# Turning the latents between two layers of a diffusion block: strided engine writes in layer 0, or a trip through DRAM at the layer boundary

## Chip, cores and metric

One core of one Trainium2 chip runs the whole program as one launch. The metric is the device time of an execution in microseconds (us); smaller is better.

## What is computed

Two layers of a hybrid diffusion block run over 512 latent tokens (a grid of 8 rows by 64 columns, read row by row) and 256 context tokens, with 1024 features each. Layer 0 mixes with gated linear attention (GLA) and a gated spatial product (gMLP); layer 1 mixes with a Mamba-2 scan (SSD) that reads the latents column by column. Each layer ends with a SwiGLU feed-forward net (FFN). The reference turns the tokens around layer 1's mixer alone:

```python
def to_col_major(x):
    bsz, t, d = x.shape
    rows = t // GRID_W
    return x.reshape(bsz, rows, GRID_W, d).transpose(0, 2, 1, 3).reshape(bsz, t, d)
...
    for i in range(DEPTH):
        ...
        hx = modulate(rms_norm(x, norm_g[i, 0]), mx[0], mx[1])
        hc = modulate(rms_norm(ctx, norm_g[i, 0]), mc[0], mc[1])
        if i % 2 == 0:
            yx, yc = mixer_gla_gmlp(hx, hc, ...)
        else:
            yx_cm, yc = mixer_ssd(to_col_major(hx), hc, ...)
            yx = to_row_major(yx_cm)
        x = x + mx[2] * yx
        x = x + mx[5] * swiglu(modulate(rms_norm(x, norm_g[i, 1]), mx[3], mx[4]), ffn_w_in[i], ffn_w_out[i])
```

Residual, norms and FFN act on each token alone, so the turn may stand at any place between layer 0's mixer and layer 1's.

## The kernel before, in words

Tokens lie in six tiles of 128: tiles 0 to 3 are latents, tiles 4 and 5 context. All products run in float16 with split operands (high x high, high x low, low x high), so three matmuls of TensorE (PE) stand for one. The program notes its operations in program order and a planner (`Plan`) puts them into an order per engine by a list schedule over its own estimated costs; PE, VectorE (DVE), ScalarE (ACT) and the one DMA queue of SyncE (SP) then run their lists in order. Nearly every instruction carries the line number of the planner's issue loop (562), so the rows below tell them apart by tile names and shapes: `area` is the big on-chip working area, `bank` a PSUM bank, `gran` and `stg` hold weights, `small` a tile's norm sums.

Layer 0 works on row-major tokens up to the ends of its two branches. There the results become the output projection's operand `aT_a` (GLA) and `aT_b` (gMLP), features in partitions and tokens in columns, in two float16 parts: ACT writes the high part, DVE the low part. The kernel before writes the latents' columns in column-major order at that point. For GLA this is one 128x512 write per engine and latent tile (4 tiles); for gMLP one per engine and block of features (4 blocks):

```python
            hi, lo = (t[:, :, XS].rearrange("p h (c r) -> p h r c", r=8)[:, :, 2 * i:2 * i + 2, :] for t in aT_a)
```

Neighbouring elements of such a write lie 8 elements, 16 bytes, apart; the context tiles, and every other write, are contiguous. The residual tiles X[0] to X[3] are loaded in column-major order, and from there on all is column-major.

Layer 0's FFN ends with a product per tile and half, 12 in all, each followed by `resid` (DVE: multiply by the gate, add to X). The tiles come in the order 0 to 5. After each pair, `norm_tiles` makes the pair's operand of layer 1, `hT3`: on ACT the sum of squares and the scaling, on DVE the reciprocal root (`rstd_of`), 16 transposes of 128x128 on PE, then modulation and the split in two parts shared by ACT and DVE. Layer 1 starts with the step sizes (`wd`, 64 wide) and group 0 of four groups: projections with `conv_tile`, whose result goes into one of two padded tiles `pads` and through five taps of a convolution on DVE, context and latents together. `Xd` keeps the residual in DRAM until layer 1's output projection.

Of the kernel before, what the change touches and what calls it, by code (L numbers as in the profile page):

```python
# [19 lines left out]
P = 128  # L20
# [17 lines left out]
class View:  # L38
    """Part of an on-chip tile: partitions p0:p1 and (count, step in bytes) per free dimension from byte off."""
# [57 lines left out]
    def host(self, fn, shape):  # L97
        """The same memory through any view of the tile itself."""
        dims = tuple((n, 0) for n in shape[1:])
        return self._with(("host", fn), p0=0, p1=shape[0], dims=dims)  # L100
# [27 lines left out]
class Base:  # L128
    """An allocated tile; whole: any two uses of it count as overlapping."""
# [24 lines left out]

class Part(Base):
    """A tile of a pool: the scheduler gives it one of the pool's slots, from its first use to its last."""
# [10 lines left out]
class Line:  # L167
    """Tiles in program order: the first one without a slot, and how many before it hold theirs."""
# [13 lines left out]
class Pool:  # L182
    """Equal slots (tile, offset), maybe shared with an earlier pool.

    A pool holds no more than `most` slots. Of these, and of the slots that pools share, so many are kept for the tiles
    that come next in program order that some operation can always go on.
    """
# [39 lines left out]
class Plan:  # L227
    """Instructions are noted in program order, ordered by a list schedule over their estimated times, then issued."""
# [68 lines left out]
    def _note(self, op, hist, box, write, pool, bank=False):  # L297
        """A use of a box depends on the earlier uses that overlap it; uses of one pool do not block each other, and of a
        PSUM bank reads do."""
# [54 lines left out]
    def schedule(self, rounds):  # L354
        """Orders the operations: list schedules by the length of what follows, then by the latest starts that the
        schedule before allows; the shortest is taken."""
# [143 lines left out]
    def _slots(self, op, t):  # L500
        """None when every tile that the operation begins can have a slot at t, else when to look again (-1: unknown)."""
# [19 lines left out]
    def _needs(self):  # L521
        """How many tiles of a pool live at once in program order, when each one begins and soon after."""
# [51 lines left out]
def tile_hybrid_block(ctx: ExitStack, tc: tile.TileContext, t_in: dict, out: bass.AP):  # L574
# [19 lines left out]
    class Ring:  # L594
        """Slots of one size, taken in turn."""
# [115 lines left out]
    def w_rows(w, f0, k0=0, slots=(None,) * 4):  # L711
        """A block of 512 columns for each of 8 slices of the contraction."""
# [4 lines left out]
    def split_pair(w, c0, c1, slots=None):  # L717
        """Two blocks of 128 columns as the rows of A: A11, A12, A22, S1 = A21 + A22, S2 = S1 - A11, S3 = A11 - A21,
        S4 = A12 - S2."""
# [40 lines left out]
    def prod_quarter(o, w, x, sl, more=False):  # L760
        """more: on top of what the bank holds, sums that other engines read or wrote among it."""
# [19 lines left out]
    # ---- 1 / sqrt(ss * scale + eps): a guess from the halved exponent, a cubic and a quadratic step in q = v y y, both  # L781
    # without the factors that the scale of v takes up; y is negative until the last step turns it ----
# [19 lines left out]
    # Rows of 32 partitions go through four column groups of the tensor engine side by side.  # L802
# [22 lines left out]
    def turned(o, n):  # L825
        """The rows of the four groups as columns: (P, group, block of 128, row)."""
# [8 lines left out]
    def mods_cols(layer, chunk, streams):  # L835
        """A chunk of the modulation as columns, the sums over the partitions on the tensor engine."""
# [27 lines left out]
    def mods_row(layer, chunk, streams):  # L864
        """A gate as a row in DRAM per stream, with the scale of the products taken out."""
# [32 lines left out]
    def turn(xs, abv, s, put):  # L898
        """Normalised pairs of tiles as modulated columns, by blocks of 128 features; one engine reads a bank."""
        xn = norm_rows(xs)  # L900
# [19 lines left out]
    def norm_tiles(xs, abv, s, hT, m):  # L920
        ts = [t2[0]((P, 2, 2, P)) for _ in range(4)]
        turn(xs, abv, s, lambda kt: ts[kt // 2][:, kt % 2])
# [3 lines left out]
    class Pairs:  # L926
        """A feature-major operand, the tokens by pairs of tiles."""
# [10 lines left out]
    class Halves:  # L938
        """A feature-major operand in the quarters of Winograd's form of Strassen's product: B11, B21, B22 and the sums
        T1 = B12 - B11, T3 = B22 - B12, T2 = B22 - T1, T4 = B21 - T2; rows halved by feature, columns by tile parity;  # L940
        the tiles by pairs."""
# [10 lines left out]
    def norm_halves(xs, abv, s, hS, m):  # L952
        t = hS.temps((P, 2, 4, 2, P))
        turn(xs, abv, s, lambda kt: t[:, kt // 4, kt % 4])
# [16 lines left out]
    c_rows = t_in["ctx"][0]  # L971

    # =============================== layer 0, mixing ===============================
# [15 lines left out]
    for i in range(NT):  # L989
        sy.dma_start(out=x_in[i], in_=t_in["x"][0][i * P:(i + 1) * P, :] if i < 4 else c_rows[(i - 4) * P:(i - 3) * P, :])  # L990
# [17 lines left out]
    def cols_early(chunk, half):  # L1008
        """Half a shift or scale of both streams: (P, stream, block of 128)."""
# [16 lines left out]
    # The loads in the order of their use: half of shift and scale, the first weights, the other half, the other chunks.  # L1026
# [50 lines left out]
    # Gates: the rows of the low rank side as high, low, high parts and ones, the weights' as high, high, low parts and biases.  # L1077
# [130 lines left out]
    # spatial gating  # L1208
# [27 lines left out]
    for j in range(4):  # L1236
        wu = w_cols(w_in, 1568 + j * P, P)
        for sl in (XS, CS):
# [6 lines left out]
            hi, lo = aT_b[0][:, j, sl], aT_b[1][:, j, sl]  # L1245
            if sl is XS:
                hi, lo = (t.rearrange("p (c r) -> p r c", r=8) for t in (hi, lo))
                u = u.rearrange("p (r c) -> p r c", r=8)
            sc.activation(out=hi, in_=u, func=AF.Copy)
            va.tensor_tensor(out=lo, in0=u, in1=hi, op=ALU.subtract)  # L1250
# [7 lines left out]
    for i in range(NT):  # L1258
# [19 lines left out]
        if i < 4:  # L1278
            src = o.rearrange("p h (a c) -> p h a c", a=2)
            hi, lo = (t[:, :, XS].rearrange("p h (c r) -> p h r c", r=8)[:, :, 2 * i:2 * i + 2, :] for t in aT_a)  # L1280
        else:
            src = o
            hi, lo = (t[:, :, TOK[i]] for t in aT_a)
        sc.activation(out=hi, in_=src, func=AF.Copy)
# [492 lines left out]
```

## Time and profile before

| | |
|---|---|
| median of 3 runs | 1633.5 us (1630.48 to 1634.7) |
| profiled execution, first to last instruction (span) | 1628.5 us |
| median less span (start, end and run-to-run difference) | 5.0 us |
| PE busy | 1576.2 us, 97% of the span |
| DVE busy | 1394.6 us, 86% |
| ACT busy | 955.8 us, 59% |
| granted TensorE clock, mean over the span | 0.991 |

The profiled execution is one execution; its span leaves out what lies ahead of the first and behind the last instruction, so its own time is 1628.5 us plus that rest. Busy time of PE is modelled from pipelined matmuls. Times in rows count from the start of the span.

### The profile page before, as it was taken

How to read it: one execution, taken by the hardware profiler on the slowest of the kernel's cores; microseconds unless marked ns; L12 is line 12 of the kernel's file. 1: busy time of each engine (PE TensorE's matmuls, PEld its weight loads, DVE VectorE, ACT ScalarE, POOL GpSimd, SP SyncE). 2: the span in 40 equal slices, each digit the busy share in tenths (PEclk: the TensorE clock that was granted, in tenths of full speed). 3: DMA queues.
4: the chain of work that ended last, by engine and by line, in shares of the span. 5: the costliest groups of instructions: out<-in, count | busy, mean ns of one | idle time of the engine just before them, and what ended most of it. 6: DMA issues, size and time to landing. Idle time of an engine off the chain costs nothing.

```text
span 1628.5 us, 28131 instructions
## 1 busy us (share of the span) xinstructions
PE 1576.2 (97%) x10893; PEld 953.9 (59%) x10893; DVE 1394.6 (86%) x2661; ACT 955.8 (59%) x1900; POOL 21.4 (1%) x65
## 2 busy tenths in 40 slices
PE   5999989999999999999999999999999999999997
PEld 4555555467545554555569555555544587686774
DVE  3899988689999988966478999999999888898775
ACT  6957437265514622623456899889986576464541
POOL 2000000000000000000000000000000000000000
PEclk8999989999999999999999999999999999999999
DMA  9763335014545566421231455445576324343311
GB/s 329 216 186 113 103 96 156 33 40 126 162 147 162 168 196 192 143 66 59 78 105 47 135 149 148 119 117 153 139 229 186 86 86 128 118 124 113 113 53 52
DMA packets 206121, 210.53 MB, mean 129 GB/s; under 512 B 27199, under 2 KB 154275, under 8 KB 205987
## 3 DMA queue, kind: packets, MB, share of 16 engines
q1 hardware_dynamic: 205987, 208.74, 42.7%
q8 instruction: 85, 1.39, 0.3%
q14 instruction: 49, 0.40, 0.1%
HBM read 197.01 MB, written 7.50 MB: 126 GB/s over the span
## 4 chain that ended last, share of the span: by engine, by line
PE 54%; DVE 23%; ACT 11%; DMA 9%; issue 3%; SPq 0%; DVEq 0%; ACTq 0%
PE bank L562 54%; DVE area L562 15%; ACT area L562 7%; DVE gran L562 5%; DMA stg<-in_ffn_w_in_dram 4%; DMA area<-in_mod_w_dram 2%; DVE stg L562 2%; ACT gran L562 2%; DVE small L562 1%; ACT L562 1%; ACT L560 1%; DMA area<-in_mod_b_dram 1%; SPq L562 0%; DMA area<-rowd 0%; DMA stg<-in_ssd_w_out_dram 0%
## 5 line engine op out<-in xcount | busy, mean ns | idle before, releaser
L562 PE MATMUL bank<-area,gran 128*128 128x256 f16 (+3 forms) x5604 | 789.2, 296 | 3.4 <-DVE area L562 1.8
L562 PEld LDWEIGHTS <-gran 128*128 128x128 f16 x5604 | 519.9, 98 | 252.1 <-issue 19.9
L562 PE MATMUL bank<-area 128*128 128x512 f16 (+9 forms) x3170 | 542.7, 328 | 10.7 <-DVE area L562 5.3
L562 PEld LDWEIGHTS <-area 128*128 128x128 f16 (+1 forms) x3270 | 303.1, 98 | 316.0 <-issue 22.9
L562 ACT ACTIVATE gran<-stg 128x512 f16<-128x512 f32 (+2 forms) x366 | 252.1, 700 | 231.5 <-PE bank L562 96.4
L562 ACT ACTIVATE area<-area 128x128 f32<-128x128 f32 (+8 forms) x557 | 254.1, 502 | 134.6 <-DVE area L562 118.8
L562 DVE TENSOR_TENSOR area<-area 128x512 f32<-128x512 f32 (+8 forms) x489 | 302.1, 641 | 22.8 <-ACT area L562 19.3
L562 ACT ACTIVATE area<-bank 128x384 f32<-128x384 f32 (+7 forms) x460 | 212.2, 482 | 175.7 <-PE bank L562 137.8
L562 DVE SCALAR_TENSOR_TENSOR gran<-stg,gran 128x512 f16<-128x512 f32 (+2 forms) x366 | 278.2, 777 | 32.8 <-ACT gran L562 32.0
L562 PE MATMUL bank<-gran,area 128*128 128x512 f16 (+1 forms) x1308 | 285.7, 361 | 2.0 <-DVE area L562 1.7
L562 DVE TENSOR_TENSOR area<-bank,area 128x512 f32<-128x512 f32 (+5 forms) x237 | 143.2, 612 | 65.1 <-PE bank L562 62.7
L562 DVE SCALAR_TENSOR_TENSOR area<-area,cs 128x512 f32<-128x512 f32 x224 | 159.9, 745 | 10.7 <-DMA area<-in_mod_w_dram 10.0
L562 PEld LDWEIGHTS bank<-area 128*64 128x64 f32 (+4 forms) x1208 | 75.2, 151 | 39.8 <-issue 15.9
L562 DVE SCALAR_TENSOR_TENSOR area<-area,mrow 128x772 f32<-128x772 f32 (+1 forms) x96 | 91.0, 970 | 0.6 <-ACT area L562 0.5
L562 ACT ACTIVATE area<-stg 128x1024 f16<-128x1024 f32 (+1 forms) x56 | 55.0, 998 | 40.1 <-PE bank L562 18.6
L562 DVE SCALAR_TENSOR_TENSOR area<-stg,area 128x1024 f16<-128x1024 f32 (+1 forms) x56 | 64.2, 1153 | 10.0 <-ACT area L562 9.7
L562 ACT ACTIVATE area<-area,small 128x64 f32<-128x64 f32 (+2 forms) x161 | 61.8, 459 | 13.9 <-DVE small L562 13.8
L562 PE MATMUL bank<-ident,area 128*128 128x128 f32 (+1 forms) x351 | 54.0, 294 | 15.3 <-DMA area<-in_ssd_norm_g_dram 5.5
L562 DVE TENSOR_TENSOR stg<-stg,stg 128x512 f32<-128x512 f32 x88 | 60.5, 687 | 1.6 <-DMA stg<-in_ffn_w_in_dram 1.0
L562 PEld LDWEIGHTS bank<-ident,area 128*128 128x128 f32 (+1 forms) x351 | 43.9, 151 | 29.1 <-POOL area L562 5.5
L562 DVE TENSOR_TENSOR stg<-stg 128x512 f32<-128x512 f32 x88 | 60.2, 685 | 0.3
L562 DVE SCALAR_TENSOR_TENSOR area<-area 64x128 f32<-64x128 f32 (+3 forms) x148 | 52.8, 400 | 4.7 <-ACT area L562 4.3
(74 smaller groups left out, 573.2 us busy)
## 6 DMA issues: line engine op xcount, KB each, us to landing
area<-in_mod_w_dram SPq DMA_DIRECT2D x96, 512.0 KB, 3.9
stg<-in_ffn_w_in_dram SPq DMA_DIRECT2D x88, 512.0 KB, 4.4
stg<-in_ffn_w_out_dram SPq DMA_DIRECT2D x44, 512.0 KB, 3.6
stg<-in_ssd_w_in_dram SPq DMA_DIRECT2D x40, 512.0 KB, 3.6
area<-rowd SPq DMA_DIRECT2D x32, 512.0 KB, 5.0
stg<-in_ab_w_in_dram SPq DMA_DIRECT2D x20, 512.0 KB
stg<-in_ssd_w_out_dram SPq DMA_DIRECT2D x32, 256.0 KB, 2.9
area<-in_x_dram SPq DMA_DIRECT2D x8, 512.0 KB, 4.6
```

Of the source, the lines that this page charges most:

```text
L560: eng.preload_act_table_set(TABLE_SETS[table])
L562: getattr(eng, method)(*map(real, a), **{n: real(v) for n, v in k.items()})
```

## The change

Layer 0's two branches write their operands contiguously, all residual tiles are loaded as they lie, and layer 0 stays row-major. The last FFN chunk of layer 0 takes the context tiles first (`last=(4, 5, 0, 1, 2, 3)`). Each finished latent tile is normalised by itself (`norm_rows`), and stored to a DRAM tensor `Xn`, its residual to `Xd`; both stores go to column-major rows (`rows(i)`: 2 grid rows of 64 tokens, 4 KB each). When all four are done, the normalised latents are loaded back as column-major tiles over X (`columns(k)`), and transposed, modulated and split in two pairs. `conv_tile` works on the context ahead of the latents. Layer 1's residual is loaded from `Xd.columns(i)`.

```diff
+class Turned(Base):
+    def _view(self, p0, p1, fn):
+        return View(self, p0, p1, 0, ((D, 4),), F32, (("host", fn),))
+
+    def rows(self, i):
+        return self._view(32 * i, 32 * i + 32, lambda ap: ap.rearrange("(c r) d -> r c d", r=8)[2 * i:2 * i + 2])
+
+    def columns(self, i):
+        return self._view(0, P, lambda ap: ap[P * i:P * i + P])
...
-    def norm_tiles(xs, abv, s, hT, m):
+    def norm_tiles(xn, abv, s, hT, m):
...
-            hi, lo = aT_b[0][:, j, sl], aT_b[1][:, j, sl]
-            if sl is XS:
-                hi, lo = (t.rearrange("p (c r) -> p r c", r=8) for t in (hi, lo))
-                u = u.rearrange("p (r c) -> p r c", r=8)
-            sc.activation(out=hi, in_=u, func=AF.Copy)
-            va.tensor_tensor(out=lo, in0=u, in1=hi, op=ALU.subtract)
+            split(u, [t[:, j, sl] for t in aT_b])
...
-        if i < 4:
-            src = o.rearrange("p h (a c) -> p h a c", a=2)
-            hi, lo = (t[:, :, XS].rearrange("p h (c r) -> p h r c", r=8)[:, :, 2 * i:2 * i + 2, :] for t in aT_a)
-        else:
-            src = o
-            hi, lo = (t[:, :, TOK[i]] for t in aT_a)
-        sc.activation(out=hi, in_=src, func=AF.Copy)
-        va.tensor_tensor(out=lo, in0=src, in1=hi, op=ALU.subtract)
+        split(o, [t[:, :, TOK[i]] for t in aT_a])
...
-        sy.dma_start(out=X[i], in_=x_cm[16 * i:16 * i + 16] if i < 4 else c_rows[(i - 4) * P:(i - 3) * P, :])
+        sy.dma_start(out=X[i], in_=x_rows(i))
...
-    Xd = [scratch((P, D), F32, f"Xd{i}") for i in range(4)]
+    Xd, Xn = (Turned(dram.tile([SEQ, D], F32, name=n)) for n in ("Xd", "Xn"))
...
-                 [k * KB for k in range(96, 120, 4)], gate5):
-        if i % 2:
-            norm_tiles(X[i - 1:i + 1], ab[1, 0], int(i >= 4), hT3, i // 2)
+                 [k * KB for k in range(96, 120, 4)], gate5, last=(4, 5, 0, 1, 2, 3)):
         if i < 4:
-            sy.dma_start(out=Xd[i], in_=X[i])
+            with pl.rushed(20.0):
+                sy.dma_start(out=Xn.rows(i), in_=norm_rows(X[i:i + 1])[0])
+            sy.dma_start(out=Xd.rows(i), in_=X[i])
+        if i == 3:
+            for k in range(4):
+                sy.dma_start(out=X[k], in_=Xn.columns(k))
+            for k in (0, 2):
+                norm_tiles(X[k:k + 2], ab[1, 0], 0, hT3, k // 2)
+        if i == 5:
+            norm_tiles(norm_rows(X[4:6]), ab[1, 0], 1, hT3, 2)
...
-        for sl, o0 in ((XS, 2), (CS, 518)) if with_ctx else ((XS, 2),):
+        for sl, o0 in ((CS, 518), (XS, 2)) if with_ctx else ((XS, 2),):
...
-        sy.dma_start(out=X[i], in_=Xd[i])
+        sy.dma_start(out=X[i], in_=Xd.columns(i))
```

What the planner makes of it stands in the order per engine. On SP's queue, at the end of layer 0's FFN, the kernel before has the four stores of the residual among weight loads:

```order
L562 DMA stg3_75<-in_ssd_w_in_dram 128x2x512
L562 DMA Xd1_124<-area_71 128x1024
L562 DMA stg1_73<-in_ssd_w_in_dram 128x8x128
L562 DMA Xd0_123<-area_71 128x1024
L562 DMA Xd2_125<-area_71 128x1024
L562 DMA area_71<-in_ssd_a_log_dram 128x64
L562 DMA Xd3_126<-area_71 128x1024
L562 DMA area_71<-in_ssd_conv_w_dram 120x128
```

At the same place the changed kernel has:

```order
L576 DMA stg1_73<-in_ssd_w_in_dram 128x8x128
L576 DMA Xd_123<-area_71 2x64x1024 x2
L576 DMA Xn_124<-area_71 2x64x1024 x2
L576 DMA Xd_123<-area_71 2x64x1024 x2
L576 DMA area_71<-in_ssd_a_log_dram 128x64
L576 DMA Xn_124<-area_71 2x64x1024 x2
L576 DMA area_71<-Xn_124 128x1024 x4
L576 DMA area_71<-in_ssd_conv_w_dram 120x128
L576 DMA stg2_74<-in_ssd_w_in_dram 128x8x128
```

The four stores and four loads of `Xn` are new, and the loads stand ahead of the next weight loads of layer 1. On PE, behind the last product of layer 0's FFN, the kernel before goes straight on to the latents of group 0's first projection (weights `gran1`):

```order
L562 LDWEIGHTS area_71
L562 MATMUL bank4_67<-area_71 128x512
L562 LDWEIGHTS gran1_77
L562 MATMUL bank7_70<-area_71,gran1_77 128x256
```

In the changed kernel the context columns of four projections (96 matmuls 256 wide) and of the step sizes (48 matmuls 64 wide) stand there, with the last transposes of the context pair ahead of them; their end, and the latents' transposes behind it, read:

```order
L576 LDWEIGHTS gran5_81
L576 MATMUL bank5_68<-area_71,gran5_81 128x256
L576 MATMUL bank4_67<-ident_94,area_71 128x128 x4
L576 MATMUL bank6_69<-ident_94,area_71 128x128 x4
L576 MATMUL bank0_63<-ident_94,area_71 128x128 x4
L576 LDWEIGHTS gran1_77
L576 MATMUL bank4_67<-area_71,gran1_77 128x256
```

All latent work of layer 1 has moved behind the transposes of the reloaded tiles, and PE has nothing else in its list between the last `gran5` matmul and those transposes.

## Rows read from the trace of the kernel before

**Rows 1.** The page: busy time of each engine.
```profile
PE 1576.2 (97%) x10893; PEld 953.9 (59%) x10893; DVE 1394.6 (86%) x2661; ACT 955.8 (59%) x1900; POOL 21.4 (1%) x65
```

**Rows 2.** Waits of PE, 160 to 300 us: total us, times, longest.
```profile
PE bank L562 <- DVE area L562: 8.6, 5, 2.7
PE bank L562 <- DVE small L562: 3.0, 2, 2.0
```

**Rows 3.** Windows of layer 0's mixer: length, busy us per engine, granted clock, DMA.
```profile
187.50:231.60 44.10, 36.59 (x340) 21.83 (x338) 41.71 (x98) 17.30 (x27) 2.64 (x5) 0.96 0.19 61
231.60:265.00 33.40, 33.40 (x206) 18.12 (x208) 25.95 (x62) 13.71 (x29) 0.53 (x1) 0.90 0.61 187
265.00:293.40 28.40, 24.30 (x142) 12.90 (x142) 24.88 (x60) 18.90 (x39) 0.00 (x0) 1.00 0.40 114
293.40:300.00 6.60, 6.60 (x23) 2.88 (x24) 2.00 (x5) 0.60 (x1) 0.00 (x0) 0.74 0.20 79
```

**Rows 4.** Groups by form, 160 to 300 us: busy us, mean ns, idle before.
```profile
L562 DVE TENSOR_TENSOR area<-bank,area 128x512 f16<-128x512 f32 x6 | 11.1, 1852 | 0.6 <-ACT area L562 0.6
L562 DVE TENSOR_TENSOR area<-area 128x512 f16<-128x512 f32 x4 | 9.8, 2448 | 0.7 <-ACT area L562 0.7
L562 ACT ACTIVATE area<-area 128x512 f16<-128x512 f32 x4 | 10.0, 2488 | 7.1 <-DVE area L562 7.1
```

**Rows 5.** Timeline of DVE: start, us, operation; a latent tile, then a context tile.
```profile
282.98 2.44 DVE L562 TENSOR_TENSOR area<-bank,area 128x512 f16<-128x512 f32 x1
...
295.28 0.69 DVE L562 TENSOR_TENSOR area<-bank,area 128x512 f16<-128x512 f32 x1 [0.57 <-ACT area L562]
```

**Rows 6.** The chain that ended last, around the last latent tile of GLA.
```profile
287.51 2.35 DVE area L562
...
293.39 6.67 PE bank L562 x22
```

**Rows 7.** Timeline of PE at the layer boundary: last FFN matmuls, first of layer 1.
```profile
838.45 5.34 PE L562 MATMUL bank<-area 128*128 128x512 f16 x24
843.63 5.73 PE L562 MATMUL bank<-area,gran 128*128 128x256 f16 x51
```

**Rows 8.** PE by form, 843 to 897 us.
```profile
L562 PE MATMUL bank<-area,gran 128*128 128x256 f16 x408 | 46.2, 273 | 0.0
L562 PE MATMUL bank<-gran,area 128*128 128x64 f16 x144 | 5.3, 193 | 0.0
L562 PE MATMUL bank<-ident,area 128*128 128x128 f32 x42 | 5.1, 272 | 0.0
```

**Rows 9.** Timelines of DVE and ACT at the boundary: residual, modulation; sum of squares, scaling.
```profile
821.52 1.34 DVE L562 TENSOR_TENSOR area<-bank,area 128x512 f32<-128x512 f32 x2 [1.40 <-PE bank L562]
...
849.84 1.91 DVE L562 TENSOR_SCALAR area<-bank,a,mc 128x256 f32<-128x256 f32 x4 [3.06 <-PE bank L562]
...
844.42 1.06 ACT L562 ACTIVATE area<-area 128x1024 bf16<-128x1024 f32 x1
...
846.81 2.19 ACT L562 ACTIVATE area<-area,small 128x1024 f32<-128x1024 f32 x2 [1.23 <-DVE small L562]
```

**Rows 10.** DMA issues: count, KB, us to landing (at 800 to 1000, 240 to 310, 0 to 24 us).
```profile
Xd<-area SPq DMA_DIRECT2D x4, 512.0 KB, 3.1
...
area<-in_x_dram SPq DMA_DIRECT2D x2, 512.0 KB, 4.6
...
area<-in_ctx_dram SPq DMA_DIRECT2D x2, 512.0 KB, 11.1
```

**Rows 11.** Windows at the program's start and in layer 1 (columns as in group 3).
```profile
10.00:20.00 10.00, 8.21 (x113) 6.11 (x117) 2.19 (x3) 2.85 (x7) 2.31 (x4) 1.00 1.04 391
...
840.00:930.00 90.00, 88.69 (x792) 68.48 (x791) 78.11 (x137) 67.71 (x121) 5.81 (x17) 1.00 0.26 77
930.00:1010.00 80.00, 79.81 (x554) 44.97 (x553) 77.98 (x128) 79.31 (x192) 0.00 (x0) 1.00 0.52 146
```

**Rows 12.** PE by form, 930 to 1200 us, where group 0 is scanned and group 1 projected.
```profile
L562 PE MATMUL bank<-area,gran 128*128 128x512 f16 x399 | 97.3, 379 | 0.0
```

More of the change, by code (lines that the diff above doesn't have):

```diff
@@ L896, in norm_rows, with turn @@
         return xn
-    def turn(xs, abv, s, put):
-        xn = norm_rows(xs)
+    def turn(xn, abv, s, put):
         a, b = abv
@@ L918, in split @@
         va.tensor_tensor(out=dst[1], in0=src, in1=dst[0], op=ALU.subtract)
-    def norm_tiles(xs, abv, s, hT, m):
+    def norm_tiles(xn, abv, s, hT, m):
         ts = [t2[0]((P, 2, 2, P)) for _ in range(4)]
-        turn(xs, abv, s, lambda kt: ts[kt // 2][:, kt % 2])
+        turn(xn, abv, s, lambda kt: ts[kt // 2][:, kt % 2])
         for t, k0 in zip(ts, range(0, KT, 2)):
@@ L953, in norm_halves @@
         t = hS.temps((P, 2, 4, 2, P))
-        turn(xs, abv, s, lambda kt: t[:, kt // 4, kt % 4])
+        turn(norm_rows(xs), abv, s, lambda kt: t[:, kt // 4, kt % 4])
         b11, b12, b21, b22 = (t[:, j, :, i] for j in range(2) for i in range(2))
@@ L970, in tile_hybrid_block, with x_rows @@
     XS, CS = slice(0, SEQ), slice(SEQ, NTOK)
-    c_rows = t_in["ctx"][0]
+    def x_rows(i):
+        return t_in["x"][0][TOK[i]] if i < 4 else t_in["ctx"][0][TOK[i - 4]]
     hT = split_tile((0, 12 * KB), KT, NTOK)
@@ L989, in tile_hybrid_block @@
     for i in range(NT):
-        sy.dma_start(out=x_in[i], in_=t_in["x"][0][i * P:(i + 1) * P, :] if i < 4 else c_rows[(i - 4) * P:(i - 3) * P, :])
+        sy.dma_start(out=x_in[i], in_=x_rows(i))
     for i0, n in ((0, 2), (2, 2), (4, 2)):
@@ L1277, in tile_hybrid_block @@
                 te.transpose(o[:, h, :], a[:, h, :], ident)
-        if i < 4:
-            src = o.rearrange("p h (a c) -> p h a c", a=2)
-            hi, lo = (t[:, :, XS].rearrange("p h (c r) -> p h r c", r=8)[:, :, 2 * i:2 * i + 2, :] for t in aT_a)
-        else:
-            src = o
-            hi, lo = (t[:, :, TOK[i]] for t in aT_a)
-        sc.activation(out=hi, in_=src, func=AF.Copy)
-        va.tensor_tensor(out=lo, in0=src, in1=hi, op=ALU.subtract)
+        split(o, [t[:, :, TOK[i]] for t in aT_a])
     X = [at(36 * KB + 4 * KB * i, (P, D)) for i in range(NT)]
     gate = {s: at(60 * KB + 4 * KB * s, (P, D)) for s in range(2)}
-    x_cm = t_in["x"][0].rearrange("(r c) d -> c r d", c=64)
     for i in range(NT):
-        sy.dma_start(out=X[i], in_=x_cm[16 * i:16 * i + 16] if i < 4 else c_rows[(i - 4) * P:(i - 3) * P, :])
+        sy.dma_start(out=X[i], in_=x_rows(i))
     for s in range(2):
@@ L1325, in tile_hybrid_block, with ffn @@
                 norm_halves(X[i - 1:i + 1], ab[0, 1], int(i >= 4), hS0, i // 2)
-    def ffn(layer, hS, parts, ntile, chunks, hids, slots, g, pieces=None, early=None, ne=0):
+    def ffn(layer, hS, parts, ntile, chunks, hids, slots, g, pieces=None, early=None, ne=0, last=None):
         w1, w2 = t_in["ffn_w_in"][layer], t_in["ffn_w_out"][layer]
@@ L1369, in ffn @@
                 wo += w_out(w2, f0 + f, 1, [slots[(f0 + f) % ns]])
-            for i in range(ntile):
+            tiles = last if last and ck == len(chunks) - 1 else range(ntile)
+            for n, i in enumerate(tiles):
                 for sl in pieces if pieces and ck == len(chunks) - 1 and i == ntile - 1 else HALF:
                     o = ring_m((P, sl.stop - sl.start))
-                    prod_tm(o, hv, i, cols(wo, sl), sooner=5.0 * (ntile - 1 - i) if ck == len(chunks) - 1 else 0.0)
+                    prod_tm(o, hv, i, cols(wo, sl), sooner=5.0 * (ntile - 1 - n) if ck == len(chunks) - 1 else 0.0)
                     resid(o, i, sl, g[int(i >= 4)])
```

## The prediction

> **What bounds the kernel now.** I read the page first. PE is busy for 97% of the span, DVE for 86% [rows 1]. So a microsecond in which PE stands still, or runs at half clock, is a microsecond of the result, and the question at each place is whether PE waits there and for whom. PE's waits in layer 0's mixer come next: 11.6 us there, nearly all of it for DVE [rows 2]. The windows show where. From 187.5 to 231.6 us DVE is busy for 41.7 of 44.1 us and PE for 36.6: DVE sets the pace. From 265.0 to 293.4 us PE lacks 4.1 us. The clock adds to it: after the waits that end at 231.6 and 293.4 us the mean granted clock is 0.90 and 0.74 of full speed, so part of these stretches ran at 1.2 instead of 2.4 GHz [rows 3].
>
> Who holds DVE there is read from the groups by form. Ten writes of float16 stand out. The four of gMLP's latents take 2.45 us on DVE (2.49 on ACT); the six of GLA average 1.85 us on DVE [rows 4]. The timeline takes that average apart: a latent tile's write takes 2.44 us, a context tile's, of the same shape but contiguous, 0.69 [rows 5]. The chain of work that ended last runs through them: 2.35 us of DVE directly before PE starts again at 293.4 us [rows 6].
>
> At the layer boundary the picture is the opposite. PE goes from layer 0's last FFN matmuls to layer 1's first projection without a gap [rows 7], and between 840 and 930 us it is busy for 88.7 of 90 us [rows 11]. All that the new round trip makes PE wait is new.
>
> **What goes: the strided writes.** Each of the eight on DVE loses 2.44 - 0.69 = 1.75 us, in all 14.0 us; ACT loses about as much and is seldom waited for. What PE gets of it goes by stretches [rows 3]:
> - 187.5 to 231.6 us holds the four of gMLP, 7.0 us. DVE keeps 34.7 us of work plus the 2.4 us that it idled, 37.1. PE's own work is 36.6 less 1.8 for the clock of 0.96, so 34.8, and DVE still sets the pace: gain 7.0 us. PE's waits shrink from 7.5 to 2.3 us in several pieces.
> - 231.6 to 265.0 us: PE is busy throughout at 0.90. If the waits ahead of it are short the clock has no reason to fall: 0.10 x 33.4 = 3.3 us.
> - 265.0 to 293.4 us holds the four of GLA. DVE's 24.9 us become 17.9, below PE's 24.3, so PE's 4.1 us of waiting go. Here order helps too: in column-major order each latent tile's write touches columns of all output tiles, contiguously it touches its own.
> - 293.4 to 300 us: 0.26 x 6.6 = 1.7 us.
>
> Sum 16.1 us. Lower bound 11.1: the clock's 5.0 us stay lost, because other short waits take the place of these. Upper bound 18.4: all idle and clock loss of these rows (7.5 + 1.8 + 3.3 + 4.1 + 1.7). I take 16.1, since DVE's surplus is what the rows name.
>
> The Trainium skill, page "SBUF — State Buffer", section "Door 1: The DMA port swizzle", says that memory lines are 16 bytes long and that one may stride "for free" as far as 8 bf16. Here the step is exactly 8 two-byte elements; read as still free, the rule would make this gain 0 and leave the loss below alone, 1633.5 + 10.6 = 1644 us. The rows time this very write at 2.44 against 0.69 us and decide, so this reading gets no chance; the page's other half, that each access to a new line pays, fits them.
>
> **What comes: the round trip.** Let T be the end of the last FFN matmul. Before, T is at about 843.7 us and no gap follows.
> - DVE's tail. In the changed list, from the multiplication of the second last finished product on (at T - 1.3 us, six matmuls of 0.22 us ahead of T by [rows 7]) stand 12 operations of 512 columns: four multiplications, four additions, four splits of the context pair. Two of them take 1.34 us with their overlap, so some 0.62 each [rows 9]: 7.5 us. One reciprocal root lies among them, about 1.3 us (in the row pair of ACT it is the time from the end of the squares at 845.5 to the scaling at 846.8). The last addition ends at T + 7.5.
> - Normalising the last tile: squares 1.06 plus 0.2 for reading the sum, root 1.3, scaling 2.19 / 2 = 1.1 [rows 9]: T + 11.2.
> - Store of 512 KB: 3.1 as the residual's stores [rows 10], 0.35 to issue: T + 14.6.
> - Loads. They wait for all four stores, and a pair of tiles is needed at once. The first lands after 3.1 (the plain stores) to 4.6 us (the column-major load of x) [rows 10]; the second adds 0.5 MB at the 391 GB/s of the busiest start window [rows 11], 1.3 us. That makes 4.4 to 5.9; I take 5.2, the middle: T + 19.8. The second pair lands 2.7 us later, behind DVE's work on the first.
> - Cover on PE: four context transposes (0.12 us each), 96 matmuls of 0.113 and 48 of 0.037 [rows 8] make 0.5 + 10.9 + 1.8 = 13.2 us.
>
> So PE idles 19.8 - 13.2 = 6.6 us. Then come transposes, modulation (0.48 us each, [rows 9]) and splits ahead of the first product; PE transposes meanwhile, so I count 1.5 us. The idle time of 2 to 2.7 us in layer 0 brought the clock down for 3.3 and 1.7 us of loss [rows 3]; I take 2.5 here. Sum 10.6 us.
>
> Lower bound 6.7: half of DVE's tail is done before T and the pair lands in 4.4, so the idle time is 4, with 1.0 and 1.7. Upper bound 18: the reload lands only after 11.1 us, as the context loads do at the program's start, where the DMA engines are full [rows 10, 11], idle 12.5, with 2 and 3.3.
>
> Is the delay paid back later? PE has some slack in the scans: 0.244 us for a 512-wide matmul [rows 12] against 0.22 where it runs dense [rows 7]. But there DVE is busy for 78.0 of 80 us [rows 11], and DVE stands still during the round trip as well (T + 11 to T + 20). I count nothing back.
>
> Costed at nothing: the four more stores and loads (4 MB on a queue that is 26% busy at 840 to 930 us [rows 11]; the weight loads behind them come some 10 us later, their slots are free only when PE has done the work that waits anyway); single roots for latent tiles instead of paired ones (small DVE operations, inside the tail above); contiguous loads of x, same size; context ahead of latents in groups 1 to 3, same work.
>
> **Sum.** 1628.5 - 16.1 + 10.6 = 1623.0 us of span; the median before lies 5.0 us above the span shown, so 1628.0.
>
> **Rivals.**
> 1. *No change.* The gain stays at 11.1 because short waits go on to pull the clock down: 11.1 - 10.6 gives 1633.0. For it: DVE keeps the pace up to 231.6 us even afterwards. Against: PE's remaining waits there are a third of today's.
> 2. *The trip is mostly hidden.* Loss 6.7, net -9.4, 1624.1. For it: DVE's tail is the least certain term, and PE has slack in the scans. Against: DVE has none there.
> 3. *Slower.* Place: SP's queue behind the last store of normalised latents. If store and reload both take the 11.1 us of the loaded start, the pair lands at T + 35 instead of T + 19.8, the loss is 26, the time 1643. It turns slower than before by more than 0.3% when store plus reload take over 18.7 us instead of 8.3 (0.3% of 1633.5 is 4.9 us, about what a measurement of this kernel can tell from no change). Against: the queue is nearly empty at that place, and the column-major load of x, whose rows of 4 KB are strided in the same way, took 4.6 us.
> 4. *The turned store crawls.* If a store that reorders rows went 19 times slower than a plain one, 3.1 would become 59 us, four of them in a row delay PE by at least that: 1680 or more. The only near row, 4.6 us for a load that reorders the same way, speaks against. The Trainium skill has such a rule, page "VectorE: DVE Perf Modes", section "The three transpose paths": a plain DMA whose access pattern does a transpose is 19x slower than the crossbar's when the innermost destination stride is large. Here the innermost 4 KB stay together, and no run has shown the case yet.
>
> **Chances.** Forecast, net -8 to -1 us (1625.5 to 1632.5): 0.48. Rival 2, below 1625.5: 0.20. Rival 1 and what else ends between 1632.5 and 1638.4: 0.20. Rival 3: 0.10, rival 4: 0.02. Faster by over 0.3% means below 1628.6: rival 2 and a little over half of the forecast, 0.46. Slower: rivals 3 and 4, 0.12. The rest, 0.42, is within 0.3%. Leaving out one in ten at each end gives 1620 to 1640, with 1625.5 to 1632.5 as the forecast's own.
>
> **What would show it.** Right: the float16 writes of the latents at 0.6 to 0.7 us on both engines; PE's waits at 160 to 300 us down from 11.6 to below 4 us and the clock at 1.00 from 231 to 300; out of the FFN's end one wait of PE for a DMA from `Xn`, 5 to 9 us long, and a stretch at half clock behind it. Wrong: PE's waits in layer 0 stay although the writes are short; or PE's wait at the boundary is under 3 or over 12 us; or the delay at the boundary is gone by the end of group 0's scan.

## The result, and the profile of the changed kernel

The changed kernel takes 1682.5 us (median of 4 runs, 1680.85 to 1683.29) against 1632.0 us (median of 4, 1628.85 to 1634.7) for the kernel before: ratio 1.0308, 95% interval 1.0292 to 1.0324. It is 50 us slower; the forecast was 1628, and its range ended at 1640.

Layer 0 did what was forecast, and a little more. The busy times of the page first, then the waits of PE at 160 to 300 us, then the windows of layer 0's mixer (columns as in [rows 3]):

```profile
PE 1569.5 (93%) x10893; PEld 951.3 (57%) x10893; DVE 1378.6 (82%) x2671; ACT 941.6 (56%) x1900; POOL 21.5 (1%) x65
```

```profile
PE bank L576 <- DVE area L576: 0.8, 3, 0.3
```

```profile
187.50:231.60 44.10, 43.15 (x367) 25.43 (x364) 41.53 (x120) 14.56 (x36) 2.64 (x5) 1.00 0.36 120
231.60:265.00 33.40, 33.40 (x232) 19.06 (x231) 26.56 (x69) 19.96 (x55) 0.53 (x1) 1.00 0.45 147
265.00:293.40 28.40, 28.40 (x137) 13.42 (x136) 17.17 (x48) 6.78 (x11) 0.00 (x0) 1.00 0.27 87
293.40:300.00 6.60, 6.60 (x41) 3.97 (x39) 3.96 (x7) 4.79 (x8) 0.00 (x0) 1.00 0.00 0
```

PE's waits of 11.6 us [rows 2] are down to 0.8, the clock of 0.90 and 0.74 [rows 3] is at 1.00, and PE is idle for 1 us in 112.5. The windows are the same times, not quite the same work: layer 0 now runs ahead, at its end by some 16 us (below). The writes behind it, by form (busy us, mean ns; answers to [rows 4]):

```profile
L576 DVE TENSOR_TENSOR area<-bank,area 128x512 f16<-128x512 f32 x6 | 4.1, 683 | 1.7 <-ACT area L576 1.7
...
L576 DVE TENSOR_TENSOR area<-area 128x512 f16<-128x512 f32 x4 | 2.7, 683 | 0.2 <-ACT area L576 0.2
```

What was lost was lost at the layer boundary. PE's waits for the reload there (total us, times, longest), then its timeline, the place of [rows 7]; the bracket is the idle time ahead of the row and what ended it:

```profile
PE bank L576 <- DMA area<-Xn: 63.5, 2, 62.7
```

```profile
829.34 5.08 PE L576 MATMUL bank<-area,gran 128*128 128x256 f16 x45
897.14 0.47 PE L576 MATMUL bank<-ident,area 128*128 128x128 f32 x1 [62.72 <-DMA area<-Xn]
```

One wait of 62.7 us for the reload of the normalised latents. The reload waits for the stores, and SP's queue shows how those went (start, time in which the group was issued):

```profile
810.60 4.63 SPq L576 DMA_DIRECT2D Xd<-area  x2
824.38 6.14 SPq L576 DMA_DIRECT2D Xn<-area  x2
830.63 19.49 SPq L576 DMA_DIRECT2D Xd<-area  x2
...
859.96 10.38 SPq L576 DMA_DIRECT2D Xn<-area  x2
893.37 1.77 SPq L576 DMA_DIRECT2D area<-Xn  x4
```

Eight stores of 512 KB, 4.19 MB, take from 810.6 to 893.4 us, 51 GB/s. A window in the middle says what kind of slowness it is (the last two columns are the busy share of the 16 DMA engines and GB/s):

```profile
840.00:842.00 2.00, 0.00 (x0) 0.00 (x0) 0.00 (x0) 0.00 (x0) 0.00 (x0) 0.50 0.12 51
```

A busy share of 0.12 with stores queued up all the time: it looks not like 16 engines doing something slow, but like about 2 of 16 doing anything; the experiments below settle it. The reload behind them moved 390 GB/s. The stores also reach back into ACT, whose scalings of the last two latent tiles wait until a store has let go of their slot:

```profile
843.52 1.15 ACT L576 ACTIVATE area<-area,small 128x1024 f32<-128x1024 f32 x1 [12.85 <-DMA Xn<-area]
853.49 1.15 ACT L576 ACTIVATE area<-area,small 128x1024 f32<-128x1024 f32 x1 [8.82 <-DMA Xn<-area]
```

So the last tile is scaled only at 854.6, 32.5 us after the last FFN matmul (T = 822.1), where the forecast had T + 11.2.

### The profile page after: what moved, and what is told of

Same layout as the page of the kernel before. It is cut to its first block, busy times and chain, and to the rows that moved or that the text cites. A ratio compares the mean times of both kernels' runs of the same rounds, so it can differ in the third digit from the quotient of the medians.

```text
span 1679.1 us, 28163 instructions
## 1 busy us (share of the span) xinstructions
PE 1569.5 (93%) x10893; PEld 951.3 (57%) x10893; DVE 1378.6 (82%) x2671; ACT 941.6 (56%) x1900; POOL 21.5 (1%) x65
## 4 chain that ended last, share of the span: by engine, by line
PE 43%; DVE 29%; DMA 14%; ACT 10%; issue 3%; SPq 1%; DVEq 0%; ACTq 0%
PE bank L576 43%; DVE area L576 19%; ACT area L576 7%; DVE gran L576 6%; DMA stg<-in_ffn_w_in_dram 5%; DMA Xn<-area 3%; DVE stg L576 3%; DMA area<-in_mod_w_dram 3%; ACT gran L576 2%; DVE small L576 1%; DMA area<-area 1%; DMA area<-in_mod_b_dram 1%; ACT L574 1%; ACT L576 1%; SPq L576 1%
## 5 line engine op out<-in xcount | busy, mean ns | idle before, releaser
L576 ACT ACTIVATE area<-area 128x128 f32<-128x128 f32 (+9 forms) x557 | 247.5, 488 | 151.1 <-DVE area L576 120.1
L576 DVE TENSOR_TENSOR area<-area 128x512 f32<-128x512 f32 (+8 forms) x489 | 294.4, 623 | 21.3 <-ACT area L576 13.9
L576 ACT ACTIVATE area<-bank 128x384 f32<-128x384 f32 (+7 forms) x460 | 205.0, 464 | 189.5 <-PE bank L576 137.2
L576 DVE TENSOR_TENSOR area<-bank,area 128x512 f32<-128x512 f32 (+5 forms) x237 | 135.3, 580 | 60.8 <-PE bank L576 55.1
L576 PE MATMUL bank<-ident,area 128*128 128x128 f32 (+1 forms) x351 | 54.0, 295 | 78.1 <-DMA area<-Xn 63.5
L576 ACT ACTIVATE area<-area,small 128x64 f32<-128x64 f32 (+1 forms) x161 | 62.1, 460 | 38.4 <-DMA Xn<-area 21.7
L576 DVE TENSOR_SCALAR area<-bank,a,mc 128x256 f32<-128x256 f32 x32 | 15.4, 538 | 80.9 <-PE bank L576 80.9
L576 DVE SCALAR_TENSOR_TENSOR area<-stg,area 128x1024 f16<-128x1024 f32 (+1 forms) x56 | 63.9, 1152 | 11.5 <-ACT area L576 11.3
```

The costliest lines, as they stand in the source:

```text
L576: getattr(eng, method)(*map(real, a), **{n: real(v) for n, v in k.items()})
```

## Experiments

**Which property of the stores is slow?** A store of the changed kernel writes 128 rows of 4 KB as a pattern of 2 x 64 x 1024. Two things set it apart from the plain store of 3.1 us [rows 10]: its slowest dimension has 2 steps, and each row of 4 KB goes to a place of its own, 32 KB from the last. The first theory blames the 2 steps, the second the scattering.

`e1_halves` cuts each store into two of 64 partitions; rows go where they went, the slowest dimension has 64 steps.

```diff
+            for j in range(2):
+                sy.dma_start(out=Xd.rows(i, j), in_=X[i][64 * j:64 * j + 64])
...
```

> The changed kernel, but each store of Xn and Xd is cut in two stores of 64 partitions (one grid row each), so that its slowest dimension has 64 steps instead of 2; the destination rows in DRAM stay the same, 4 KB every 32 KB. Theory A, the slowest dimension of 2 puts a store on 2 of the 16 DMA engines: stores land in 3 to 5 us, PE's wait for Xn falls from 62.7 to 5 to 9 us, time 1620 to 1630 us. Theory B, the scattered destination rows make the store crawl: nothing changes, 1675 to 1690 us, and the DMA share between the FFN's end and the reload stays at 0.1.

Measured: 1629.95 us, ratio 0.9984 (0.9973 to 0.9995). PE's waits at the boundary (790 to 930 us), its timeline, the scaling of the last tiles on ACT, and the stores of `Xn` (count, KB, us to landing):

```profile
PE bank L577 <- DMA area<-Xn: 10.3, 3, 8.9
```

```profile
820.28 2.75 PE L577 MATMUL bank<-area 128*128 128x512 f16 x12
...
830.28 5.08 PE L577 MATMUL bank<-area,gran 128*128 128x256 f16 x45
844.27 0.47 PE L577 MATMUL bank<-ident,area 128*128 128x128 f32 x1 [8.91 <-DMA area<-Xn]
845.65 3.37 PE L577 MATMUL bank<-ident,area 128*128 128x128 f32 x16 [0.91 <-DMA area<-Xn]
```

```profile
831.89 2.41 ACT L577 ACTIVATE area<-area,small 128x1024 f32<-128x1024 f32 x2 [0.29 <-DVE small L577]
```

```profile
Xn<-area SPq DMA_DIRECT2D x8, 256.0 KB, 2.9
```

Theory A names the time, at the upper end of its range; PE's wait, 10.3 us, is longer than the 5 to 9 expected. The 53 us by which PE waits less (63.5 us for `Xn` in all before this edit, 10.3 after it) are the 53 us between the profiled spans, 1679.1 and 1626.0.

`e5_two_long_runs` does the reverse: 2 steps, but each writes 64 neighbouring rows, 256 KB in one piece, into a padded DRAM tensor; the turn is left to the loads.

```diff
+        return self._view(32 * i, 32 * i + 32, lambda ap: ap[2 * i:2 * i + 2, 0:64])
...
+    Xd, Xn = (Turned(dram.tile([8, 72, D], F32, name=n)) for n in ("Xd", "Xn"))
...
```

> The changed kernel, with stores that keep their slowest dimension of 2 steps but go to long runs: each step writes 64 neighbouring rows, 256 KB in one run (the DRAM tensor holds 72 rows per grid row so that the two steps stay apart); the loads turn. Theory A (2 of 16 engines): as slow as the changed kernel, 1675 to 1690 us, PE's wait for Xn over 50 us, DMA share 0.1 to 0.13 meanwhile. Theory B (scattered rows): 1620 to 1630 us.

Measured: 1688.3 us, ratio 1.0342 (1.0324 to 1.036), with the same waiting and the same engine share in the window of 840 to 842 us:

```profile
PE bank L576 <- DMA area<-Xn: 66.4, 3, 63.9
```

```profile
840.00:842.00 2.00, 0.00 (x0) 0.00 (x0) 0.00 (x0) 0.00 (x0) 0.00 (x0) 0.87 0.13 53
```

Scattered rows with many steps are fast, long runs with two steps are slow: the second theory has fallen.

**Is the number of steps the number of engines?** `e13_four_steps` and `e14_eight_steps` are this kernel with 4 steps of 32 rows and 8 of 16; the edit with 4:

```diff
+        return self._view(32 * i, 32 * i + 32, lambda ap: ap[4 * i:4 * i + 4, 0:32])
...
```

> As e5_two_long_runs, but each store's slowest dimension has 4 steps of 32 rows (128 KB in one piece each) in place of 2. If the number of steps is the number of engines that carry a store, the eight stores (4 MB) go at about twice the 53 GB/s of the changed kernel, 106 GB/s, and take 40 us instead of 79 from their start at 811; the last is on its way until about 852, PE idles for the latents some 20 to 25 us (62.7 in the changed kernel), and the time is 1638 to 1648 us. Rival: a slowest dimension shorter than 16 puts the store on the same few engines whatever its length; then it is 1680 to 1690 us again. Second rival: what limits is one engine's share of rows in a run, so that 4 steps are enough; then it is 1630 us as with 16 or more.

> The same with 8 steps of 16 rows. If steps are engines, the stores go at about 212 GB/s, 2.5 us each; they then no longer queue up behind each other for long (the last two normalised tiles come 1.2 us apart), and PE idles 9 to 14 us: 1629 to 1635 us. Rival (same few engines whatever the length): 1680 to 1690 us.

Measured: 1649.1 us (ratio 1.0118, 1.0083 to 1.0154) and 1639.9 us (1.0064, 1.0044 to 1.0084). The same window of 840 to 842 us and PE's waits, first with 4 steps, then with 8:

```profile
840.00:842.00 2.00, 0.00 (x0) 0.00 (x0) 0.00 (x0) 1.67 (x2) 0.00 (x0) 0.50 0.25 104
PE bank L576 <- DMA area<-Xn: 32.7, 3, 29.9
```

```profile
840.00:842.00 2.00, 0.00 (x0) 0.00 (x0) 0.00 (x0) 0.00 (x0) 0.00 (x0) 0.50 0.51 211
PE bank L576 <- DMA area<-Xn: 17.8, 3, 15.3
```

2, 4 and 8 steps: busy shares of 0.13, 0.25 and 0.51, that is 2, 4 and 8 of 16 engines, and 53, 104 and 211 GB/s, some 26 GB/s for each. The trace's single DMA packets agree: in that window the 4 KB packets of the changed kernel take 159 ns each, and two are under way at a time; with 4 and 8 steps it is mostly four and eight. The expectations' rivals, the same few engines at any length and 4 steps being enough, have fallen. The times came out above the expectation (PE waited 32.7 and 17.8 us for `Xn` where 20 to 25 and 9 to 14 were expected). The rate alone doesn't count the slots that stores hold: ACT's last scalings waited for one 4.0 and 3.8 us with 4 steps, and 2.6 us with 8, which is part of the excess.

The Trainium skill, page "DMA: Bandwidth & Descriptors", section "Rules for kernel authors", states this rule: the number of engines follows the slowest dimension of more than one step, and one with fewer than 16 "confines the whole DMA to at most c engines". By that rule an estimate of the shares is 0.125, 0.25 and 0.5 for 2, 4 and 8 steps; the traces agree.

**Do slow stores delay fast ones?** `e10_xn_halves_only` halves the stores of `Xn` and leaves the residual's four at 2 steps.

```diff
+                for j in range(2):
+                    sy.dma_start(out=Xn.half(i, j), in_=xn[64 * j:64 * j + 64])
             sy.dma_start(out=Xd.rows(i), in_=X[i])
...
```

> The changed kernel with only the normalised tiles' stores cut into halves of 64 partitions; the four residual stores keep their slowest dimension of 2. If each store's own engines are all that matters, the latents come back as in e1_halves, and it takes about 1630 us. If slow residual stores on 2 engines hold up what is queued behind them (8 x 256 KB of halves have descriptors on those 2 engines too; the four residual stores carry 2 MB, at 53 GB/s 39 us), the latents are back 25 to 40 us late and it takes 1650 to 1670 us.

Measured: 1648.9 us, ratio 1.0121 (1.0105 to 1.0137). PE's wait for `Xn`, and the landing of the halves:

```profile
PE bank L580 <- DMA area<-Xn: 28.6, 2, 27.8
Xn<-area SPq DMA_DIRECT2D x8, 256.0 KB, 10.3
```

The halves of `Xn`, stored as in `e1_halves`, land after 10.3 us instead of 2.9. The second theory holds, with less than it expected: PE waits 18.3 us longer than in `e1_halves`, not 25 to 40, and the profiled spans lie 19.8 us apart (1645.8 and 1626.0). Stores that nobody waits for before layer 1's end cost 18 to 20 us by what they hold up behind them.

**The two halves of the change, each alone.** `e2_turn_on_load` has all of the change, with plain stores; the loads turn, with 16 steps outermost. `e3_no_turn` is the kernel before with contiguous writes in layer 0 and no trip; it leaves out the turn of the latents. `e4_trip_alone` is the kernel before with a trip that turns nothing and with the context tiles first. The edit of `e2_turn_on_load`:

```diff
-        return self._view(32 * i, 32 * i + 32, lambda ap: ap.rearrange("(c r) d -> r c d", r=8)[2 * i:2 * i + 2])
+        return self._view(32 * i, 32 * i + 32, lambda ap: ap[P * i:P * i + P])
...
-        return self._view(0, P, lambda ap: ap[P * i:P * i + P])
+        return self._view(0, P, lambda ap: ap.rearrange("(r c) d -> c r d", c=64)[16 * i:16 * i + 16])
```

> The changed kernel, but tiles are stored as they lie (one contiguous 512 KB run of 128 rows) and turned by the loads, whose slowest dimension has 16 steps. Both theories A and B: stores land in about 3 us, PE's wait for Xn 5 to 9 us, time 1620 to 1630 us. If it is over 3 us faster or slower than the version with stores of 64 partitions, the direction in which the rows are scattered matters as well.

> The kernel before, with layer 0's strided writes made contiguous and nothing else changed but that: no trip through DRAM, the order of tiles and of conv_tile as before. It leaves out the turn of GLA's and gMLP's latents, so layer 1 scans a mixture of orders; all work and sizes are the same. It times the gain alone. By the sum of the prediction 16.1 us (11.1 to 18.4): 1616 us (1613.5 to 1621). If the writes were not what held PE, within 5 us of the kernel before, 1627 to 1637.

> Layer 0 as in the kernel before (strided writes, column-major order), with normalise, plain store, plain reload and context tiles first added between the layers: a trip that turns nothing, on 16 engines. It prices the trip alone. If the trip costs what the profiled spans of e1_halves and e3_no_turn say (1626.0 - 1615.6 = 10.4 us), it runs at about 1643 us; if what their medians say (1630.0 - 1613.5 = 16.5 us), at about 1649 us. Rival: the gain of layer 0 and the trip's loss are not independent (part of what e3_no_turn won was won at the boundary); then it comes out under 1640 us.

| | no trip | trip on 16 engines |
|---|---|---|
| strided writes in layer 0 | kernel before: 1; span 1628.5 | `e4_trip_alone`: 1.0088 (1.0075 to 1.0102); span 1640.2; median 1644.1 |
| contiguous writes | `e3_no_turn`: 0.988 (0.9865 to 0.9894); span 1615.6; median 1613.5 | `e2_turn_on_load`: 1.0001 (0.9988 to 1.0015); span 1626.9; median 1630.8 |

`e2_turn_on_load` lies just above the expected 1620 to 1630 us, and with 0.8 us between their medians it and `e1_halves` do not tell the directions of scattering apart; `e3_no_turn` lies at the fast end of its range; `e4_trip_alone` is near the first of its two values by its time, between them by its loss (14.4 us against the kernel before in the same session, 1629.7 us; 10.4 or 16.5 were expected), and its rival, under 1640 us, has fallen.

By the spans the gain is 12.9 us without and 13.3 with the trip, the trip costs 11.7 and 11.3. By the ratios the gain is 1.2 or 0.9%, the trip 0.9 or 1.2%, so 14 to 20 us each. The two ways differ since the profiled execution is the slowest of its four in `e3_no_turn` (1617.3 us) and the fastest of its twelve in `e2_turn_on_load` (1628.65). In the latter the longer executions have the lower granted clock, 0.993 at 1628.65 us and 0.988 at 1637.25; in `e3_no_turn` all four have 0.996, and what sets them apart is open. T, the end of the last FFN matmul, measures layer 0 without what follows. The last FFN rows of the timelines of `e2_turn_on_load`, `e4_trip_alone` and `e3_no_turn`:

```profile
820.40 2.75 PE L576 MATMUL bank<-area 128*128 128x512 f16 x12
```

```profile
836.92 2.75 PE L576 MATMUL bank<-area 128*128 128x512 f16 x12
```

```profile
821.73 5.34 PE L562 MATMUL bank<-area 128*128 128x512 f16 x24
```

With the trip T is at 839.7 and 823.2, 16.5 us apart; without it at 843.8 [rows 7] and 827.1, 16.7 apart.

The two trips of the table are not the same. Where nothing is turned, a tile's reload needs that tile's store alone; where the trip turns, it needs all four. PE's first latent transposes in `e4_trip_alone`:

```profile
857.41 0.47 PE L576 MATMUL bank<-ident,area 128*128 128x128 f32 x1 [5.42 <-DMA area<-Xn]
858.68 4.51 PE L576 MATMUL bank<-ident,area 128*128 128x128 f32 x23 [0.79 <-DMA area<-Xn]
```

PE waits 6.2 us here, 11.6 in `e2_turn_on_load`. That both trips cost the same by the spans is therefore no proof that gain and loss are independent; what makes up the difference in `e4_trip_alone` is open.

**Can the trip be hidden or spared?** `e9_latents_first_plain` is `e2_turn_on_load` with the latents ahead of the context in the last FFN chunk and five slots for normalised tiles.

```diff
+    t4[0] = ring(AR, 4*KB, 5)
...
-                 [k * KB for k in range(96, 120, 4)], gate5, last=(4, 5, 0, 1, 2, 3)):
+                 [k * KB for k in range(96, 120, 4)], gate5):
...
```

> Plain stores and turning loads as in e2_turn_on_load, but the last chunk of layer 0's FFN does the latent tiles first and the two context tiles last, with five slots for normalised tiles; the first convolution block takes the latents ahead of the context. The context tiles' four products (about 13 us) then lie over the trip. If the cover is only exchanged (13 us of context products after the trip's start instead of before), PE still idles 6 to 10 us for the latents or the context and it takes 1627 to 1633 us. Rival: with both the context's feed-forward and its own first products beside the trip the idle time goes, and it takes 1618 to 1622 us.

Measured: 1627.2 us, ratio 0.9987 (0.9976 to 0.9997). PE still waits 9.0 us for `Xn`, in three pieces; the longest:

```profile
814.66 5.78 PE L576 MATMUL bank<-area 128*128 128x512 f16 x26
827.02 0.45 PE L576 MATMUL bank<-ident,area 128*128 128x128 f32 x1 [6.58 <-DMA area<-Xn]
```

The cover was exchanged, as the first theory said, with the time and the wait that it gave: the context's FFN products now lie over the trip, and its layer 1 products, which did before, come later.

`e11_direct` has no trip: copies of 16 partitions from each normalised tile straight to every eighth partition of four on-chip tiles.

```diff
+                    for k in range(4):
+                        for j in range(2):
+                            sy.dma_start(out=put(k, 2 * n + j), in_=x[64 * j + 16 * k:64 * j + 16 * k + 16])
...
```

> No trip through DRAM for the normalised latents: each normalised row tile goes by copies of 16 partitions (64 KB) straight to every eighth partition of four column tiles in on-chip memory that the context tiles and the first two latent tiles have left; only the last row tile's 8 copies are late. The residual's stores are plain and its loads turn, as in e2_turn_on_load. If the store and the reload one after the other are what PE waits for (scaled at T+11.4, first latents at T+21 to T+23 in e1_halves), one hop of 8 x 0.35 us of issue and about 3 us of landing brings them by T+17, the idle time falls from 10 us to 3 to 5 us, and it takes 1619 to 1624 us, faster than both kernels. Rival: 32 copies cost SP near 1 us each, as the halves' issues in e1_halves (4.1 us for four); the latents are then later than T+23 and it takes 1632 to 1640 us.

Measured: 1684.8 us, ratio 1.0345 (1.0327 to 1.0363). Both expectations missed. The copies land in 2.3 us each, but they go in ones and twos: PE waits for a copy's landing, and the next copies wait for PE's matmuls behind it, 48.8 us of waiting on PE in all (SP's queue, then PE):

```profile
855.32 42.40 SPq L576 DMA_DIRECT2D area<-area  x20
```

```profile
861.56 0.82 PE L576 MATMUL bank<-area,gran 128*128 128x256 f16 x3 [2.94 <-DMA area<-area]
865.35 0.82 PE L576 MATMUL bank<-area,gran 128*128 128x256 f16 x3 [2.97 <-DMA area<-area]
```

The instructions themselves carry these waits. The order of SP's queue, with the semaphores that a row waits for (PE: finished work of PE; DMAHW: an earlier DMA on the same one of eight semaphores):

```
255 L576 DMA area<-area 16x1024 [waits DMAHW0_49,PE_49,Activation_49]
256 L576 DMA area<-area 16x1024 [waits DMAHW1_49,PE_49]
257 L576 DMA area<-area 16x1024 [waits DMAHW2_49]
258 L576 DMA area<-area 16x1024 [waits DMAHW3_49,PE_49]
```

All on-chip memory involved is one allocation (`area`), and copies with a step of eight partitions were ordered against PE's reads of other places in it (the rows above are products of the context). So this run says nothing on what such copies cost when nothing orders them; with an allocation of their own it wasn't tried.

`e12_turn_in_psum` spares the trip in another way: the transposes on PE, needed anyway, write a tile's 128 columns at a step of 8 elements, so that a bank holds 512 columns in column-major order. The residual goes as in `e2_turn_on_load`.

```diff
+            o = ring_s((P, 512))
+            oc = o.rearrange("p (c r) -> p r c", r=8)
+            with pl.together():
+                for i in range(4):
+                    te.transpose(oc[:, 2 * i:2 * i + 2], xn[i][:, kt * P:(kt + 1) * P], ident)
...
```

> No trip and no copies for the normalised latents: the four normalised row tiles are kept, and TensorE's transposes, which are needed anyway, write each tile's 128 columns into the bank at a step of 8 elements (32 bytes), so that a bank holds 512 columns in column-major order. The residual is stored plainly and turned by its loads. If what costs in e1_halves and e2_turn_on_load is the store and reload behind the last scaling (T+11.4), the transposes begin there, before PE's other work ends (T+13), the idle time of 9 to 12 us goes, and the time is that of e3_no_turn with at most 4 us more: 1613 to 1618 us, faster than both kernels. Rival: TensorE's writes at a step of 32 bytes, or the evictions now made by feature block instead of by pair, take as much longer as the strided writes on VectorE did in the kernel before (3.5 times: 32 transposes at 0.19 us would take 15 us more): 1625 to 1632 us.

Measured: 1626.2 us, ratio 0.9962 (0.9949 to 0.9975), by its ratio the best version that computes the layers, 0.4% ahead of the kernel before; by the spans it is 0.8 us ahead of `e9_latents_first_plain` (1621.6 and 1622.4). PE's waits at 790 to 930 us, PE's transposes and the reads of their banks by form at 838 to 848 us, and the window of the boundary:

```profile
PE bank L576 <- ACT area L576: 2.8, 2, 2.3
PE bank L576 <- DVE area L576: 0.9, 1, 0.9
```

```profile
L576 PE MATMUL bank<-ident,area 128*128 128x128 f32 x32 | 4.3, 273 | 0.0
L576 DVE TENSOR_SCALAR area<-bank,a,mc 128x512 f32<-128x512 f32 x4 | 3.2, 811 | 4.4 <-PE bank L576 3.8 <-ACT area L576 0.5
L576 ACT ACTIVATE area<-bank,mc,a 128x512 f32<-128x512 f32 x4 | 3.1, 778 | 3.8 <-PE bank L576 3.8
```

```profile
823.00:850.00 27.00, 23.34 (x230) 20.20 (x228) 19.99 (x50) 20.25 (x33) 0.00 (x0) 0.94 0.12 45
```

The waiting for DMA is gone and 3.7 us for the context's normalising are left. The rival's time came, but not by its mechanism: the strided transposes take 273 ns as the contiguous ones did [rows 8], and the eight evictions of 512 columns take 0.81 and 0.78 us, each less than two of 256 columns together in `e1_halves` (0.54 us each on DVE, 0.57 on ACT). Idle time and clock (0.06 x 27 = 1.6 us) make 5.3 of the 6.0 us between the profiled spans of this kernel and of `e3_no_turn` (1621.6 and 1615.6); the medians lie 12.7 us apart, which is open for the same reason as above.

## Why the prediction was wrong

**The failed step** is "Store of 512 KB: 3.1 as the residual's stores", and with it "Costed at nothing: the four more stores". The price was taken from a row of the same size, not of the same pattern. What told them apart stood in the order of SP's queue, printed ahead of the prediction: `128x1024` before, `2x64x1024` after. The eight stores share 2 engines at 53 GB/s, 10 us for 512 KB (worked out) in place of 3.1, and behind each other 83 us; PE waited 63.5 us for `Xn` where 6.6 had been forecast. It is the step count that decides and not the scattering (`e1_halves`, `e5_two_long_runs`, `e13_four_steps`, `e14_eight_steps`), and the residual's stores, which nobody waits for, alone cost 18 to 20 us (`e10_xn_halves_only`).

**The rivals.** Rival 4 named the time, 1680 or more, with a chance of 0.02, and its mechanism was another: its factor of 19 compares with the crossbar's transposes and not with a plain store, and a turning store as such isn't slow: `e1_halves` turns with stores whose landing takes 2.9 us. The row that spoke against it, 4.6 us for the load of x, turns in a pattern with 16 steps outermost; it is near in what it does and far in the one thing that counts. Rival 3 had the place, SP's queue behind the last store, and its deciding point of 18.7 us for store and reload was passed by far (from the scaling's end at 854.6 to the transposes at 897.1 us); its 11.1 us would have covered one such store alone (10 us) and the reload (3.8 us from 893.4 to the transposes); what it left out is the queue of stores ahead, by which the last one took from 854.6 to 893.4, 39 us.

**What held.** The gain: 16.1 us forecast, 16.5 and 16.7 by T. Some 3.5 us of it are no longer there at the end of the profiled spans (12.9 and 13.3). They go behind T: from there to the end it takes 784.7 us in the kernel before and 788.5 in `e3_no_turn`, with PE as busy (768.0 and 768.7 us); which waits grow wasn't followed. Clock and waits in layer 0 followed the stretches as written, only PE's remaining wait up to 231.6 us, 1.0 us, is shorter than the 2.3 expected, though DVE is as busy there as before, 41.5 us: work from behind 231.6 us has moved into that window. DVE's tail and the normalising: forecast T + 11.2; in `e1_halves` the last scaling ends at 834.3, T + 11.3.

**The trip on 16 engines** was costed at 10.6 us, bounds 6.7 to 18; it measures 11.3 to 11.7 by spans, and 12.2 to 16.6 us by the interval of `e4_trip_alone`. In `e1_halves` two pieces were off, both towards a longer wait. From the last scaling to the issue of the reload it takes 6.6 us (T + 11.3 to T + 17.9) instead of 3.4, so that the pair of latents is there at T + 22.6 instead of T + 19.8; and PE's cover ends at T + 12.3 instead of 13.2. PE waits 10.3 us instead of 6.6. In `e4_trip_alone`, where a reload needs one store, the pair is there at T + 19.0 and PE waits 6.2 us. The lower bound was also mis-summed: half of DVE's tail and a pair in 4.4 us leave 2.0 us of idle time, not 4, and 4.7 in all instead of 6.7. So with stores on 16 engines the change is worth 1.6 us by the profiled spans with plain stores (1628.5 to 1626.9) and 2.5 with halved ones (to 1626.0), where gain less loss had been forecast at 5.5; by the ratios, 1.0001 and 0.9984, it is worth nothing that shows and 0.2%.

**What would have helped:** to ask of each new transfer not only how many bytes it moves but how many steps its outermost dimension has, and to give the unknown pattern an upper bound from its own shape. No row of the trace of before showed an outermost dimension under 16 of this size, so the bound had to be wide.

## What to carry to other kernels

Read the outermost dimension of every DMA pattern first: below 16 steps it bought only that share of the engines here, and cutting a transfer of two steps in two, so that the partitions come first, costs one more issue and wins the rest. A slow transfer that nobody waits for still holds slots and the queue behind it. Before sending data through memory to reorder it, look whether an operation that is needed anyway can write the new order: here PE's transposes into their bank do so at the same 273 ns.

## What was not expected of the hardware

- A store from on-chip memory to DRAM whose pattern is led by 2, 4 or 8 steps moves 53, 104 and 211 GB/s (engine shares 0.13, 0.25, 0.51), some 26 GB/s per step.
- Rows of 4 KB that go to places 32 KB apart cost a store nothing that shows: 2.9 us to landing for 256 KB in `e1_halves`, and the same end-to-end time as plain stores with turning loads (1629.95 and 1630.79 us).
- PE writes transposed columns at a step of 8 float32 elements in 273 ns each, like contiguous ones [rows 8], where DVE's float16 writes at a step of 8 elements took 2.44 instead of 0.69 us [rows 5].
- During the 62.7 us of waiting PE's clock is granted at 0.50, 1.2 GHz, from 840 us on at the latest. In `e1_halves` its mean is 0.52 from 838 to 847 us, with PE's first transpose at 844.27, and 1.00 from 850 us on:

```profile
838.00:847.00 9.00, 1.83 (x8) 1.54 (x9) 0.41 (x1) 0.26 (x1) 0.00 (x0) 0.52 0.76 264
847.00:850.00 3.00, 2.50 (x15) 2.26 (x14) 2.29 (x6) 2.56 (x6) 0.00 (x0) 0.74 0.40 146
850.00:860.00 10.00, 9.52 (x88) 8.50 (x87) 6.36 (x13) 6.06 (x13) 0.75 (x1) 1.00 0.00 0
```
